# An encoder block on one core: the second norm's sum of squares moved to the end, and the operands of x made two blocks ahead

## The chip, the cores and the metric

One core of a Trainium2 chip runs the whole kernel. The metric is the device time of one execution in microseconds (us). Three runs of the kernel before took 1968.86, 1969.41 and 1969.3 us, median 1969.3 us. A further execution, the profiled one, took 1969.88 us, of which the profile's span from the first to the last instruction is 1968.2 us.

## What is computed

The input x is 512 tokens by 2048 channels in float32. Cut to what matters here:

```
u = rms_norm(x, mix_pre_gain)
p = u @ W_in                       (2048 x 5120)
mixed = concat(short gated convolution, conformer convolution with LayerNorm)
o = mixed @ W_out                  (2048 x 2048)
h = x + rms_norm(o, mix_post_gain)
m = rms_norm(h, mlp_pre_gain)      <- the second norm of this text
z = relu(m @ W_up)^2               (2048 x 8192)
out = h + rms_norm(z @ W_down, mlp_post_gain)
```

An rms_norm divides each token by the root of its mean square over the 2048 channels. This factor is one number per token, so it can be applied after a matmul. For the second norm it comes out as r^2 behind the square of the ReLU; the kernel multiplies by it only at the very end, as r^2 (`norm_2`) on the result and r^4 (`norm_4`) on the mean square under the last root.

## The kernel before, in words

Up to the last stage everything lies with channels across the 128 partitions and the 512 tokens along the free dimension; there are 16 blocks (k) of 128 channels. Each float32 operand is split into a high and a low part (`split`, lines 92 to 100: ScalarE writes the high part, VectorE the rest), and each product of two operands is three matmuls. Weights are split the same way by `Stationary.prepare` (lines 230 to 246: ScalarE line 237, VectorE line 242) from raw tiles of 128 x 1024 that the SP queue loads (line 122); there are six raw tiles. The order of instructions on every engine is the program's order (a manual schedule). All engines work through their own queue in that order.

**The first stage** is `k_major` (line 318) with `mixer_input` (line 448): four output tiles (PSUM banks) grow together, block by block of x. Per block k: x is split (lines 97 and 98), for even k below 8 a quarter of the first four weight tiles is cut into high and low parts (`cut_pieces`, lines 94 and 95), ScalarE squares x (line 409) and GpSimd adds the square to a running sum (line 405). From block 4 on, weight tiles 4 to 7, which are wanted from block 8 on, are prepared, one per block, behind the block's own operands. `together` (lines 309 to 316) issues twelve matmuls of 512 columns per block, three for each tile. `load_x` (line 442) loads a block of x four blocks ahead into one of eight buffers `tmp`, which x shares with the squares.

**The start of the MLP** (lines 729 to 760) does the same for h. Six blocks are done by half of the tokens; from block 6 on whole blocks follow. `residual` (lines 692 and 694, VectorE) makes h from x and o, `mlp_split` (lines 97 and 98) splits it, `together` multiplies it with the first four tiles of W_up. `keep_h` (line 710), up to two per block, writes h to memory, makes a scaled copy on ScalarE (line 713), and adds the square of h to `h_sum` (square on ScalarE line 409, sum on GpSimd lines 403 and 405). In blocks 12 to 15 one weight tile is prepared in each.

Behind it, in the first run of deferred work, `h_norm` (line 771) sums `h_sum` over the partitions by a matmul with ones (line 380) and takes the root.

**The last stage** has tokens across the partitions. Its last chunk works on tiles of 512 output channels (`wide_tile`, line 893): four banks, one per 128 tokens, four blocks, that is two steps of 24 matmuls. After each step `last_step` turns two pieces of h with four TensorE transposes each into one bank (`turn`, line 1005) and ScalarE copies the bank out (line 1013). `turn_norm` (line 997) turns r^2 the same way ahead of this. There are seven banks in all. After the four tiles, the second half of the chunk is worked row by row (line 1085), 128 tokens at a time, and each row ends with `last_sum`, `root` and `write`.

Of the kernel before, what the change touches and what calls it, by code (L numbers as in the profile page):

```python
# [8 lines left out]
F32 = mybir.dt.float32  # L9
F32R = mybir.dt.float32r  # L10
AF = mybir.ActivationFunctionType
ALU = mybir.AluOpType

P = 128
S = 512
TOK = S // 2
D = 2048
DA = 1024
FF = 8192
EPS = 1e-6  # L20
KT = D // P
# [9 lines left out]
START = 4  # L31
# [4 lines left out]
N_WIDE = D // WIDE  # L36
TB = S // P
# [21 lines left out]
def encoder_block(  # L59
    ctx: ExitStack, tc: tile.TileContext, x, par, gain, w_in, w_out, w_up, w_down, out  # L60
):
    nc = tc.nc
    pool = lambda name, bufs, **kw: ctx.enter_context(tc.tile_pool(name=name, bufs=bufs, **kw))
    const = pool("const", 1)
    stats = pool("stats", 2)
    small = pool("small", 12)
# [10 lines left out]
    new = lambda p, shape, dt, tag: p.tile(shape, dt, name=f"{tag}_{next(serial)}", tag=tag)  # L77
    scratch = lambda cols=S: new(tmp, [P, cols], F32, "tmp")
    slot = lambda shape, dt=F32: new(slots, shape, dt, "slot")
    bank = lambda cols=S: new(psum, [P, cols], F32, "bank")  # L80
# [6 lines left out]
    eps = const.tile([P, 1], F32, name="eps")  # L87
    nc.gpsimd.memset(eps, EPS)
    warm = const.tile([P, 1], F32, name="warm")
# [208 lines left out]
    def block(part, b):  # L298
        return tuple(w[:, b * P : (b + 1) * P] for w in part)

    def both(pair, cols=slice(0, S)):
        return pair[:, 0, cols], pair[:, 1, cols]

    def full_tile(parts, moving):
        ps = bank()
        products(ps, [(block(parts[k // HALF], k % HALF), both(moving[k])) for k in range(KT)])
        return ps

    def together(pss, parts, b, moving, first, last, cols=slice(0, S)):

        mhi, mlo = both(moving, cols)
        for ps, part in zip(pss, parts):
            hi, lo = block(part, b)
            nc.tensor.matmul(ps[:, cols], hi, mhi, start=first, stop=False)  # L314
            nc.tensor.matmul(ps[:, cols], lo, mhi, start=False, stop=False)  # L315
            nc.tensor.matmul(ps[:, cols], hi, mlo, start=False, stop=last)  # L316

    def k_major(n, make_moving, blocks=KT):

        pss = [bank() for _ in range(n)]  # L320
        for k in range(blocks):
            b = k % HALF
            if b == 0:
                parts = W.take(n, 0)
            moving = make_moving(k)
            if HALF // 2 <= b and b - HALF // 2 < n:
                W.prepare(W.taken + b - HALF // 2 + 1)
            together(pss, parts, b, moving, k == 0, k == blocks - 1)
        return pss

    lower, upper, every = slice(0, TOK), slice(TOK, S), slice(0, S)
    add = lambda out, a, b, op=ALU.add: nc.vector.tensor_tensor(out, a, b, op=op)  # L332
    pending = deque()

    def run_pending():
        while pending:
            pending.popleft()()
# [38 lines left out]
    def column_sums(tiles, cols=S):  # L376

        ps = new(psum_stat, [P, S], F32, "sums")
        for n, t in enumerate(tiles):
            nc.tensor.matmul(ps[:, :cols], ones, t, start=n == 0, stop=n == len(tiles) - 1)  # L380
        return ps[:, :cols]

    def inverse_root(ps, count, cols=S, out=None):

        y, v = scratch(cols), scratch(cols)
        nc.scalar.activation(y, ps, AF.Abs_reciprocal_sqrt, scale=1.0 / count, bias=eps)
        nc.vector.tensor_scalar(
            out=v, in0=ps, scalar1=1.0 / count, scalar2=EPS, op0=ALU.mult, op1=ALU.add
        )
        nc.vector.scalar_tensor_tensor(out=v, in0=v, scalar=-0.5, in1=y, op0=ALU.mult, op1=ALU.mult)  # L390
        nc.vector.tensor_tensor(v, v, y, op=ALU.mult)
        r = new(stats, [P, cols], F32, "rstd") if out is None else out
        nc.vector.scalar_tensor_tensor(out=r, in0=v, scalar=1.5, in1=y, op0=ALU.add, op1=ALU.mult)
        return r

    class Sum:
# [3 lines left out]
        def add(self, t):  # L400
            if self.total is None:
                self.total = new(stats, [P, self.cols], F32, "sum")
                nc.gpsimd.tensor_copy(self.total, t)
            else:
                nc.gpsimd.tensor_tensor(self.total, self.total, t, op=ALU.add)  # L405
# [55 lines left out]
    nc.scalar.dma_start(par_sb[:, KT:], par[:, KT:])  # L461
    W.load(START + 2)
    u = []
    pss = k_major(START, mixer_input)
    W.ahead = 5
    x_sums = column_sums([x_sum.total])
    for name, n in (("conv_b_w", TAPS_B * NB), ("ln_b_gain", NB), ("ln_b_bias", NB)):
        t = par_sb[:, _PAR[name] : _PAR[name] + n]
# [3 lines left out]
    norm = {}  # L472
# [115 lines left out]
    for kind, j, m in in_plan[START:]:  # L588
        parts = W.take(2, 2)
        run_pending()  # L590
        pump_sums()
        ps = full_tile(parts, u)
# [45 lines left out]
    pss = k_major(START, mixed_input)  # L638
    for m, ps in enumerate(pss):
        evacuate(keep_output, m, ps, scratch())  # L640
    for m in range(START, OUT_SEVEN[0]):
        parts = W.take(2, 2)
        run_pending()
        ps = full_tile(parts, mixed)
# [7 lines left out]


    h_dram = dram.tile([P, KT * S], F32, name="h_dram")
    h_sum = Sum()
    xr, rstd_o, mlp_in = [], {"all": new(stats, [P, S], F32, "rstd")}, {}

    def load_xr(k):
# [51 lines left out]
    def keep_h(k):  # L710
        h = xr[k // 2][:, k % 2, :]
        nc.scalar.dma_start(h_dram[:, k * S : (k + 1) * S], h)
        nc.scalar.activation(o[k], h, AF.Copy, scale=col("mlp_pre_gain", k))
        h_sum.add_square(h)

    parts = W.take(4, START)
    run_pending()
# [12 lines left out]
    parts = W.take(START, 0)  # L730
    pss = [bank() for _ in range(START)]
# [16 lines left out]
    for k in range(HEAD, KT):  # L748
        b = k % HALF
        if b == 0:  # L750
            parts = W.take(START, 0)
# [13 lines left out]
    def relu_squared(m, value, out):  # L765

        nc.scalar.activation(out, value, AF.Relu)
        nc.scalar.activation(out, out, AF.Square)
        nc.scalar.dma_start(z_dram[:, m * S : (m + 1) * S], out)

    def h_norm():
        r = inverse_root(column_sums([h_sum.total]), D)
        norm["h 2"], norm["h 4"] = r, new(stats, [P, S], F32, "rstd")
        nc.vector.tensor_tensor(r, r, r, op=ALU.mult)
        nc.vector.tensor_tensor(norm["h 4"], r, r, op=ALU.mult)

    t12, t3, t4 = [], [], []

    def right_sums(i):
# [25 lines left out]
        "t4": lambda i: both(mlp_in[2 * i], upper),  # L805
    }

    late = [h_norm] + [lambda m=m, ps=ps: relu_squared(m, ps, scratch()) for m, ps in enumerate(pss)]
    for m in range(START, UP_PLAIN):
        parts = W.take(2, 2)  # L810
        run_pending()
        ps = full_tile(parts, mlp_in)
        pending.extend(late)
        late = []
        pending.append(lambda m=m, ps=ps: relu_squared(m, ps, scratch()))
        n = HALF // (UP_PLAIN - START)
# [74 lines left out]
    tokens = lambda n: slice(n * P, (n + 1) * P)  # L891
# [60 lines left out]
    for c in range(N_CHUNK - 1):  # L952
        sums, waiting = deque(range(CHUNK // 2)), []
# [26 lines left out]
    identity = scratch(P)  # L980
    nc.gpsimd.memset(identity, 1.0)
    nc.gpsimd.affine_select(
        out=identity, in_=identity, pattern=[[1, P]], compare_op=ALU.is_equal, fill=0.0, base=0,
        channel_multiplier=-1,
    )
    norm_2, norm_4 = (new(small, [P, TB], F32, "four") for _ in range(2))
    h_raw, h_back = {}, {}

    def load_h(t):
# [4 lines left out]
            )  # L994
            h_raw[t, 2 * n], h_raw[t, 2 * n + 1] = pair[:, 0, :], pair[:, 1, :]

    def turn_norm():
        ps = bank()
        for b in range(TB):
            nc.tensor.transpose(ps[:, tokens(b)], norm["h 2"][:, tokens(b)], identity)  # L1000
        for b in range(TB):
            nc.scalar.activation(norm_2[:, b : b + 1], ps[:, b * P : b * P + 1], AF.Copy)
        add(norm_4, norm_2, norm_2, ALU.mult)

    def turn(t, b):

        if b % 2 == 0:
            pair = slot([P, 2, WIDE])
            h_back[t, b], h_back[t, b + 1] = pair[:, 0, :], pair[:, 1, :]
        ps = bank()  # L1010
        for i in range(4):
            nc.tensor.transpose(ps[:, tokens(i)], h_raw[t, i][:, tokens(b)], identity)  # L1012
        nc.scalar.activation(h_back[t, b], ps, AF.Copy)

    turns = deque((t, b) for t in range(N_WIDE) for b in range(TB))

# [8 lines left out]

    load_h(0)
    load_h(1)
    turn_norm()
    at = (N_CHUNK - 1) * CHUNK
    for t in range(N_WIDE):  # L1030
        wide_tile(t, False, range(at, at + CHUNK // 2), chunk_block, last_step)
# [9 lines left out]
    parts = {}  # L1041
# [1 line left out]
        for n in range(CHUNK // 4):  # L1043
            (parts[t, n],) = W.take(1, 1)
    run_pending()
    nc.scalar.activation(warm, eps, AF.Abs_reciprocal_sqrt)
    sums = [new(small, [P, N_WIDE], F32, "four") for b in range(TB)]

    def last_sum(b, t, ps, gained):
        v = total[t, b]  # L1050
# [4 lines left out]
        add(gained[t], v, gains[t // 2][:, t % 2, :], ALU.mult)  # L1055

    def root(b):
        mean, y, v, r = (new(small, [P, N_WIDE], F32, "four")[:, :1] for _ in range(4))
        nc.vector.tensor_reduce(out=mean, in_=sums[b], op=ALU.add, axis=mybir.AxisListType.X)
        add(mean, mean, norm_4[:, b : b + 1], ALU.mult)  # L1060
        nc.scalar.activation(y, mean, AF.Abs_reciprocal_sqrt, scale=1.0 / D, bias=eps)
        nc.vector.tensor_scalar(
            out=v, in0=mean, scalar1=1.0 / D, scalar2=EPS, op0=ALU.mult, op1=ALU.add
        )
        nc.vector.scalar_tensor_tensor(
            out=v, in0=v, scalar=-0.5, in1=y, op0=ALU.mult, op1=ALU.mult
        )
        nc.vector.tensor_tensor(v, v, y, op=ALU.mult)
        nc.vector.scalar_tensor_tensor(out=r, in0=v, scalar=1.5, in1=y, op0=ALU.add, op1=ALU.mult)
        add(r, r, norm_2[:, b : b + 1], ALU.mult)  # L1070
        return r

# [12 lines left out]
    for b in range(TB):  # L1085
        gained = {}
        for t in range(N_WIDE):
            run_pending()
            ps = bank()
            for i in range(CHUNK // 2):  # L1090
                k = CHUNK // 2 + i
# [88 lines left out]
```

## Time and profile before

| what | value |
|---|---|
| median of three runs | 1969.3 us |
| the profiled execution | 1969.88 us |
| its span | 1968.2 us |
| TensorE (matmul) busy | 1940.5 us, 99% |
| VectorE busy | 1542.1 us, 78% |
| ScalarE busy | 815.5 us, 41% |
| GpSimd busy | 99.8 us, 5% |
| share of TensorE in the chain that ended last | 95% |
| mean granted TensorE clock | 0.996 |

A matmul is pipelined and its end is modelled, so the durations of neighbours overlap: the pace is read from the starts. A DMA row tells the time of its issue, not of its landing. "Idle before" is the time in which an engine had nothing to do ahead of an instruction, and the name behind the arrow is what ended it.

### The profile page before, as it was taken

To read this page: it belongs to the slowest core of one execution; us is meant where nothing else is said; L and a number is where in the kernel's file an instruction comes from. 1 tells how busy PE (TensorE), PEld (TensorE's weight loads), DVE (VectorE), ACT (ScalarE), POOL (GpSimd) and SP (SyncE) were. 2 spreads that over 40 slices of the span, in tenths; PEclk is the share of its full clock that TensorE was granted. 3 is DMA by queue.
4 is the path that set the end of the run, shared out by engine and by line. 5 is a ranking of instruction groups with operands and counts; after the bars stand their busy time and mean duration, and the time that the engine had idled before them with its cause. 6 is when DMAs were issued, how large, how long until landed. Compare 5 with 4: busy or idle time off the path is not lost.

```text
span 1968.2 us, 28036 instructions
## 1 busy us (share of the span) xinstructions
PE 1940.5 (99%) x11224; PEld 1717.5 (87%) x11224; DVE 1542.1 (78%) x2000; ACT 815.5 (41%) x1091; POOL 99.8 (5%) x86
## 2 busy tenths in 40 slices
PE   8999999999999899999999999999999999999998
PEld 6888888888999689999999999988888888888886
DVE  7899989668786978777777777766777777777858
ACT  6222112353444654545444544546343333433332
POOL 4000010300210400000000000000000000000000
PEclk9999999999999999999999999999999999999999
DMA  8232323232446533434334343456262453634632
GB/s 255 86 112 86 107 86 107 87 117 75 125 145 228 189 123 113 160 109 145 124 124 145 111 158 108 161 182 207 81 225 99 158 187 111 216 102 155 218 124 86
DMA packets 85523, 272.54 MB, mean 138 GB/s; under 512 B 9616, under 2 KB 11792, under 8 KB 85392
## 3 DMA queue, kind: packets, MB, share of 16 engines
q1 hardware_dynamic: 71568, 245.92, 37.4%
q10 hardware_dynamic: 13824, 24.82, 3.3%
q8 instruction: 88, 1.44, 0.3%
q14 instruction: 43, 0.35, 0.0%
HBM read 241.87 MB, written 28.84 MB: 138 GB/s over the span
## 4 chain that ended last, share of the span: by engine, by line
PE 95%; DVE 3%; DMA 1%; issue 0%; ACT 0%; SPq 0%; ACTq 0%; DVEq 0%
PE bank L296 57%; PE bank L888 11%; PE bank L889 11%; PE bank L887 11%; PE bank L316 2%; PE bank L315 2%; PE bank L314 1%; DVE slot L694 1%; DVE slot L692 1%; DMA raw<-w_in_in 0%; DVE slot L242 0%; PE bank L1012 0%; PE sums L380 0%; DVE slot L98 0%; DMA tmp<-x_in 0%
## 5 line engine op out<-in xcount | busy, mean ns | idle before, releaser
L296 PE MATMUL bank<-slot,slot 128*128 128x256 f32 (+1 forms) x7584 | 1128.2, 311 | 0.0
L296 PEld LDWEIGHTS bank<-slot,slot 128*128 128x128 f32 x7584 | 1047.0, 191 | 80.6 <-issue 1.9
L242 DVE TENSOR_TENSOR slot<-raw,slot 128x1024 fp32r<-128x1024 f32 x332 | 412.7, 1260 | 57.0 <-ACT slot L237 50.7
L237 ACT ACTIVATE slot<-raw 128x1024 fp32r<-128x1024 f32 x332 | 338.0, 1049 | 143.2 <-DVE raw L212 67.4
L887 PE MATMUL bank<-slot,slot 128*128 128x512 f32 x968 | 377.6, 390 | 0.1
L888 PE MATMUL bank<-slot,slot 128*128 128x512 f32 x968 | 376.7, 389 | 0.2 <-DVE slot L95 0.2
L889 PE MATMUL bank<-slot,slot 128*128 128x512 f32 x968 | 376.8, 389 | 0.0
L237 ACT ACTIVATE slot<-slot 128x1024 fp32r<-128x1024 f32 x170 | 176.8, 1056 | 284.3 <-PE bank L296 161.1
L242 DVE TENSOR_TENSOR slot<-slot,slot 128x1024 fp32r<-128x1024 f32 x170 | 210.8, 1240 | 56.7 <-PE bank L887 38.5
L888 PEld LDWEIGHTS bank<-slot,slot 128*128 128x128 f32 x968 | 181.7, 188 | 38.0 <-DVE slot L95 0.5
L889 PEld LDWEIGHTS bank<-slot,slot 128*128 128x128 f32 x968 | 181.7, 188 | 37.8
L887 PEld LDWEIGHTS bank<-slot,slot 128*128 128x128 f32 x968 | 181.7, 188 | 37.7 <-ACT slot L94 0.3
L332 DVE TENSOR_TENSOR tmp<-tmp,bank 128x256 f32<-128x256 f32 x224 | 93.8, 419 | 112.5 <-PE bank L296 111.4
L94 ACT ACTIVATE slot<-tmp 128x512 fp32r<-128x512 f32 x96 | 54.1, 607 | 274.6 <-DVE tmp L332 144.3
L498 DVE SCALAR_TENSOR_TENSOR slot<-slot,par_sb,slot 128x512 f32<-128x512 f32 x240 | 162.9, 742 | 0.0
L332 DVE TENSOR_TENSOR slot<-slot,bank 128x512 f32<-128x512 f32 x164 | 106.0, 681 | 22.2 <-PE bank L889 22.1
L316 PE MATMUL bank<-slot,slot 128*128 128x512 f32 (+1 forms) x216 | 82.4, 381 | 9.6 <-DVE slot L98 9.6
L314 PE MATMUL bank<-slot,slot 128*128 128x512 f32 (+1 forms) x216 | 82.3, 381 | 8.0 <-ACT slot L94 8.0
L95 DVE TENSOR_TENSOR slot<-slot,slot 128x512 fp32r<-128x512 f32 (+1 forms) x80 | 49.6, 659 | 45.6 <-ACT slot L94 45.6
L405 POOL TENSOR_TENSOR sum<-sum,tmp 128x512 f32<-128x512 f32 x50 | 77.7, 1554 | 118.4 <-ACT tmp L409 116.9
L315 PE MATMUL bank<-slot,slot 128*128 128x512 f32 (+1 forms) x216 | 81.5, 377 | 0.3 <-DVE slot L95 0.3
L165 DVE TENSOR_TENSOR slot<-raw,raw 128x1024 f32<-128x1024 f32 x64 | 78.0, 1219 | 0.0
(102 smaller groups left out, 961.1 us busy)
## 6 DMA issues: line engine op xcount, KB each, us to landing
raw<-w_up_in SPq DMA_DIRECT2D x128, 512.0 KB, 5.3
raw<-w_down_in SPq DMA_DIRECT2D x128, 512.0 KB, 4.6
raw<-w_in_in SPq DMA_DIRECT2D x76, 512.0 KB, 4.0
slot<-z_dram SPq DMA_DIRECT2D x60, 512.0 KB, 6.4
raw<-w_out_in SPq DMA_DIRECT2D x32, 512.0 KB, 4.3
z_dram<-tmp ACTq DMA_DIRECT2D x64, 256.0 KB, 5.4
tmp<-x_in SPq DMA_DIRECT2D x16, 256.0 KB, 4.1
slot<-x_in SPq DMA_DIRECT2D x8, 512.0 KB, 7.6
```

The lines of the kernel that those rows point to most:

```text
L165: nc.vector.tensor_tensor(s[name], a, b, op=op)
L237: nc.scalar.activation(hi, value, AF.Copy)
L242: nc.vector.tensor_tensor(lo, value, hi.bitcast(F32), op=ALU.subtract)
L296: nc.tensor.matmul(ps, s, m, start=n == 0, stop=n == len(todo) - 1)
L314: nc.tensor.matmul(ps[:, cols], hi, mhi, start=first, stop=False)
L315: nc.tensor.matmul(ps[:, cols], lo, mhi, start=False, stop=False)
L316: nc.tensor.matmul(ps[:, cols], hi, mlo, start=False, stop=last)
L332: add = lambda out, a, b, op=ALU.add: nc.vector.tensor_tensor(out, a, b, op=op)
L498: nc.vector.scalar_tensor_tensor(out=acc, in0=g[:, k : k + S], scalar=w, in1=acc, op0=ALU.mult, op1=ALU.add)
L887: nc.tensor.matmul(ps, z_hi, lo, start=first, stop=False)
L888: nc.tensor.matmul(ps, z_lo, hi, start=False, stop=False)
L889: nc.tensor.matmul(ps, z_hi, hi, start=False, stop=last)
```

## The change

The second norm: `keep_h` no longer squares and sums h, and `h_norm` and `turn_norm` go. In `turn`, ScalarE, besides the copy, squares the turned bank with an accumulated sum into one column of `h_sums`. Ahead of the rows these 16 columns are summed, and the root is taken by small VectorE operations (`narrow_root`, whose code was in `root` and now serves both).

The first stage: `k_major` gets a parameter `lead`. With `lead=2`, as the first stage calls it, the operands of blocks k+1 and k+2 are issued ahead of the matmuls of block k and ahead of its preparation of a weight tile. The call for W_out keeps a lead of 0.

```diff
-    def k_major(n, make_moving, blocks=KT):
+    def k_major(n, make_moving, lead=0):
-        pss = [bank() for _ in range(n)]
-        for k in range(blocks):
+        pss, made = [bank() for _ in range(n)], []
+        for k in range(KT):
             b = k % HALF
             if b == 0:
                 parts = W.take(n, 0)
-            moving = make_moving(k)
+            while len(made) < min(k + 1 + lead, KT):
+                made.append(make_moving(len(made)))
+            moving = made[k]
             if HALF // 2 <= b and b - HALF // 2 < n:
                 W.prepare(W.taken + b - HALF // 2 + 1)
...
-    pss = k_major(START, mixer_input)
+    pss = k_major(START, mixer_input, 2)
...
         nc.scalar.activation(o[k], h, AF.Copy, scale=col("mlp_pre_gain", k))
-        h_sum.add_square(h)
...
-    def h_norm():
-        r = inverse_root(column_sums([h_sum.total]), D)
-        norm["h 2"], norm["h 4"] = r, new(stats, [P, S], F32, "rstd")
-        nc.vector.tensor_tensor(r, r, r, op=ALU.mult)
-        nc.vector.tensor_tensor(norm["h 4"], r, r, op=ALU.mult)
...
+    h_sums = scratch(TB * N_WIDE)
...
-    def turn_norm():
-        ps = bank()
-        for b in range(TB):
-            nc.tensor.transpose(ps[:, tokens(b)], norm["h 2"][:, tokens(b)], identity)
-        for b in range(TB):
-            nc.scalar.activation(norm_2[:, b : b + 1], ps[:, b * P : b * P + 1], AF.Copy)
-        add(norm_4, norm_2, norm_2, ALU.mult)
...
         nc.scalar.activation(h_back[t, b], ps, AF.Copy)
+        at = b * N_WIDE + t
+        nc.scalar.activation(scratch(), ps, AF.Square, accum_out=h_sums[:, at : at + 1])
...
-    nc.scalar.activation(warm, eps, AF.Abs_reciprocal_sqrt)
...
+    def narrow_root(mean):
+        y, v = (new(small, [P, N_WIDE], F32, "four")[:, : mean.shape[-1]] for _ in range(2))
+        nc.scalar.activation(y, mean, AF.Abs_reciprocal_sqrt, scale=1.0 / D, bias=eps)
...
+    norm_2, norm_4, h_mean = (new(small, [P, TB], F32, "four") for _ in range(3))
+    over_tiles(h_mean, h_sums.rearrange("p (b t) -> p b t", b=TB))
+    h_root = narrow_root(h_mean)
+    add(norm_2, h_root, h_root, ALU.mult)
+    add(norm_4, norm_2, norm_2, ALU.mult)
```

## Rows read from the trace of the kernel before

**Rows 1.** TensorE's timeline, start of the MLP, whole blocks: start us, us, instruction.

```profile
646.08 0.39 PE L314 MATMUL bank<-slot,slot 128*128 128x512 f32 x1
...
669.60 0.80 PE L316 MATMUL bank<-slot,slot 128*128 128x512 f32 x1 [3.03 <-DVE slot L98]
...
675.31 0.41 PE L314 MATMUL bank<-slot,slot 128*128 128x512 f32 x1
...
682.84 11.04 PE L296 MATMUL bank<-slot,slot 128*128 128x512 f32 x48
```

**Rows 2.** VectorE by line and shape, 639.4 to 643.5 us: busy us, mean ns.

```profile
L242 DVE TENSOR_TENSOR slot<-raw,slot 128x1024 fp32r<-128x1024 f32 x2 | 2.4, 1218 | 0.0
L692 DVE TENSOR_TENSOR slot<-slot,rstd 128x512 f32<-128x512 f32 x2 | 1.4, 685 | 0.0
L694 DVE SCALAR_TENSOR_TENSOR slot<-slot,par_sb,slot 128x512 f32<-128x512 f32 x1 | 0.7, 746 | 0.0
L98 DVE SCALAR_TENSOR_TENSOR slot<-slot,par_sb,slot 128x512 fp32r<-128x512 f32 x1 | 0.7, 746 | 0.0
```

**Rows 3.** The same view, 644.5 to 664.8 us.

```profile
L694 DVE SCALAR_TENSOR_TENSOR slot<-slot,par_sb,slot 128x512 f32<-128x512 f32 x6 | 10.0, 1663 | 0.0
L692 DVE TENSOR_TENSOR slot<-slot,rstd 128x512 f32<-128x512 f32 x5 | 8.9, 1779 | 0.0
L98 DVE SCALAR_TENSOR_TENSOR slot<-slot,par_sb,slot 128x512 fp32r<-128x512 f32 x5 | 3.7, 739 | 0.0
```

**Rows 4.** GpSimd's timeline in that stretch.

```profile
646.67 3.19 POOL L405 TENSOR_TENSOR sum<-sum,tmp 128x512 f32<-128x512 f32 x2 [0.88 <-ACT tmp L409]
```

**Rows 5.** ScalarE by line, 644.5 to 664.8 us: busy us, mean ns, idle before.

```profile
L97 ACT ACTIVATE slot<-slot,par_sb 128x512 fp32r<-128x512 f32 x5 | 3.6, 725 | 4.8 <-DVE slot L694 4.8
```

**Rows 6.** The chain that ended last, in order of time: start us, us, what.

```profile
693.88 0.86 PE sums L380 x2
...
1863.98 0.44 PE bank L1000 x4
```

**Rows 7.** TensorE's timeline in the first stage.

```profile
24.21 0.39 PE L316 MATMUL bank<-slot,slot 128*128 128x512 f32 x1
...
30.33 0.39 PE L316 MATMUL bank<-slot,slot 128*128 128x512 f32 x1
```

**Rows 8.** ScalarE's timeline in the first stage.

```profile
24.42 1.06 ACT L237 ACTIVATE slot<-raw 128x1024 fp32r<-128x1024 f32 x1 [2.90 <-DMA raw<-w_in_in]
```

**Rows 9.** Loads of x blocks 5 to 8: first and last issue, time to landing.

```profile
L442 SPq DMA_DIRECT2D tmp<-x_in x4: 430/546/608, 13.3 to 15.1; - x4
DMA to landing us min/median/max: 6.7/6.8/6.9
```

**Rows 10.** VectorE's timeline in the first stage.

```profile
26.79 1.42 DVE L95 TENSOR_TENSOR slot<-raw,slot 128x256 fp32r<-128x256 f32 x4
...
31.02 2.32 DVE L242 TENSOR_TENSOR slot<-raw,slot 128x1024 fp32r<-128x1024 f32 x1
33.26 7.57 DVE L98 SCALAR_TENSOR_TENSOR slot<-tmp,par_sb,slot 128x512 fp32r<-128x512 f32 x5
```

**Rows 11.** TensorE's timeline at the end of a wide tile.

```profile
1888.79 1.03 PE L1012 MATMUL bank<-tmp,slot 128*128 128x128 f32 x8
...
1890.35 0.39 PE L887 MATMUL bank<-slot,slot 128*128 128x512 f32 x1
...
1891.03 0.39 PE L887 MATMUL bank<-slot,slot 128*128 128x512 f32 x1
```

**Rows 12.** ScalarE's timeline, the same turn, and a square with accumulated sum in the rows.

```profile
1889.42 1.09 ACT L1013 ACTIVATE slot<-bank 128x512 f32<-128x512 f32 x2 [4.33 <-PE bank L1012]
...
1923.46 0.64 ACT L1053 ACTIVATE tmp<-slot 128x512 f32<-128x512 f32 x1 [4.57 <-DVE slot L332]
1924.00 0.19 ACT L1053 ACTIVATION_READ_ACCUMULATOR tmp<-slot 128x1 f32 x1
```

**Rows 13.** VectorE's timeline, first tile of the last row.

```profile
1950.63 0.69 DVE L332 TENSOR_TENSOR slot<-slot,bank 128x512 f32<-128x512 f32 x1 [1.28 <-PE bank L889]
```

More of the change, by code (lines that the diff above doesn't have):

```diff
@@ L324, in k_major @@
                 parts = W.take(n, 0)
-            moving = make_moving(k)
+            while len(made) < min(k + 1 + lead, KT):
+                made.append(make_moving(len(made)))
+            moving = made[k]
             if HALF // 2 <= b and b - HALF // 2 < n:
                 W.prepare(W.taken + b - HALF // 2 + 1)
-            together(pss, parts, b, moving, k == 0, k == blocks - 1)
+            together(pss, parts, b, moving, k == 0, k == KT - 1)
         return pss
@@ L654, in encoder_block @@
     h_dram = dram.tile([P, KT * S], F32, name="h_dram")
-    h_sum = Sum()
     xr, rstd_o, mlp_in = [], {"all": new(stats, [P, S], F32, "rstd")}, {}
@@ L806, in encoder_block @@
     }
-    late = [h_norm] + [lambda m=m, ps=ps: relu_squared(m, ps, scratch()) for m, ps in enumerate(pss)]
+    late = [lambda m=m, ps=ps: relu_squared(m, ps, scratch()) for m, ps in enumerate(pss)]
     for m in range(START, UP_PLAIN):
@@ L985, in encoder_block @@
     )
-    norm_2, norm_4 = (new(small, [P, TB], F32, "four") for _ in range(2))
+    h_sums = scratch(TB * N_WIDE)
     h_raw, h_back = {}, {}
@@ L1027, in encoder_block @@
     load_h(1)
-    turn_norm()
     at = (N_CHUNK - 1) * CHUNK
@@ L1045, in encoder_block, with over_tiles @@
     run_pending()
-    nc.scalar.activation(warm, eps, AF.Abs_reciprocal_sqrt)
     sums = [new(small, [P, N_WIDE], F32, "four") for b in range(TB)]
+    def narrow_root(mean):
+        y, v = (new(small, [P, N_WIDE], F32, "four")[:, : mean.shape[-1]] for _ in range(2))
+        nc.scalar.activation(y, mean, AF.Abs_reciprocal_sqrt, scale=1.0 / D, bias=eps)
+        nc.vector.tensor_scalar(
+            out=v, in0=mean, scalar1=1.0 / D, scalar2=EPS, op0=ALU.mult, op1=ALU.add
+        )
+        nc.vector.scalar_tensor_tensor(
+            out=v, in0=v, scalar=-0.5, in1=y, op0=ALU.mult, op1=ALU.mult
+        )
+        add(v, v, y, ALU.mult)
+        nc.vector.scalar_tensor_tensor(out=v, in0=v, scalar=1.5, in1=y, op0=ALU.add, op1=ALU.mult)
+        return v
+    def over_tiles(out, sums):
+        nc.vector.tensor_reduce(out=out, in_=sums, op=ALU.add, axis=mybir.AxisListType.X)
+    norm_2, norm_4, h_mean = (new(small, [P, TB], F32, "four") for _ in range(3))
[3 more added lines that the diff above has]
+    add(norm_4, norm_2, norm_2, ALU.mult)
     def last_sum(b, t, ps, gained):
@@ L1057, in root @@
     def root(b):
-        mean, y, v, r = (new(small, [P, N_WIDE], F32, "four")[:, :1] for _ in range(4))
-        nc.vector.tensor_reduce(out=mean, in_=sums[b], op=ALU.add, axis=mybir.AxisListType.X)
+        mean = new(small, [P, N_WIDE], F32, "four")[:, :1]
+        over_tiles(mean, sums[b])
         add(mean, mean, norm_4[:, b : b + 1], ALU.mult)
[L1061 to L1069, printed above, removed]
+        r = narrow_root(mean)
         add(r, r, norm_2[:, b : b + 1], ALU.mult)
```

## The prediction

> **What bounds the kernel now.** I read the table of busy shares first: TensorE is busy 99% of the span, so the change can only gain where it takes matmuls away or closes one of the few stretches in which matmuls do not follow each other at full pace. I looked for these in TensorE's timeline. At full clock, in a stretch without waits, 33 matmuls of 512 columns start between 675.31 and 682.84 us, 0.228 us each [rows 1]. There are two slow stretches.
>
> At the start of the MLP, blocks 7 to 15 are nine blocks of twelve matmuls, 108 in all. They take from 646.08 to 682.84, 36.76 us, where 108 x 0.228 = 24.6 us would do [rows 1]. So 12.1 us are lost there. What ends the longest wait is VectorE's line 98, the low part of h. VectorE has no idle time in this stretch [rows 3], so it sets the pace. Per block it does lines 692, 98 and 694. While GpSimd is still, these take 0.69, 0.75 and 0.75 us [rows 2]; in the slow stretch line 692 takes 1.78 us and line 694 1.66 us, and line 98 alone stays at 0.74 [rows 3]. GpSimd's sums of squares come two at a time for 3.19 us with 0.88 us of rest before [rows 4]; line 98 falls into the rest. So each sum of h costs VectorE about 1.78 - 0.69 = 1.09 us.
>
> In the first stage, 72 matmuls (six blocks) have started by 24.21 us, and the ninth after it starts at 30.33 [rows 7]: 6.12 us for nine steps of 0.228, 4.1 us lost. ScalarE waits there for the DMA of a raw weight tile until 24.42 [rows 8], and the parts of x block 6 are queued behind it.
>
> **The change, part by part.**
>
> *The sums of h at the MLP's start go* (16 squares on ScalarE, 16 GpSimd operations). The squares were not on the path: ScalarE idled before line 97 waiting for VectorE [rows 5]. The GpSimd sums were on it, through VectorE. Without them a block of VectorE is at most 0.75 + 0.73 (ScalarE's line 97, longer than line 692 that runs beside it) + 0.75 = 2.23 us [rows 2, 5], against 12 x 0.228 = 2.74 us of matmuls. TensorE becomes the bound. Blocks 7 to 11 gain VectorE 5 x 0.5 = 2.5 us of lead. Blocks 12 to 15 carry a weight tile's low part, 1.22 us [rows 2]: 0.69 + 0.75 + 0.75 + 1.22 = 3.41, that is 4 x 0.67 = 2.7 us of lead used up, so it is just enough. I take the whole 12.1 us. Bounds: 12.1 us, and 6.7 us, if TensorE waits out all 2.7 us of blocks 12 to 15 and the clock falls behind that wait once more (2.75 us, below).
>
> *`h_norm` goes*: one sum over the partitions on TensorE, 0.86 us [rows 6]. Its root on ScalarE and VectorE held up nobody on TensorE: nothing.
>
> *`turn_norm` goes*: four transposes, 0.44 us [rows 6]. Its four copies and one product are beside the matmuls: nothing.
>
> *Sixteen squares with an accumulated sum come into the last stage*, two per step. Each is 0.54 us to its read of the accumulator and 0.19 us for that, 0.73 us [rows 12]; ScalarE idles 4.33 us per step before the copies [rows 12], so its own time is covered. If the cover were gone it would be 16 x 0.73 = 11.7 us. What is not covered is the bank: it is free only after the square. There are seven banks, four belong to the tile, and if they are handed out in the order in which they come free, the next tile's second and third banks are those of the last two turns. At the tile end at 1888.79 the next tile wants its second bank at 1890.35 and its third at 1891.03 [rows 11]. The first copy starts at 1889.42 and two take 1.09 [rows 12]. With the square behind each copy the first bank is free at 1889.42 + 0.55 + 0.73 = 1890.70, 0.35 us late, and the second 1.28 us later at 1891.98, against 1891.03 + 0.35 = 1891.38: 0.60 us late. That is 0.95 us at each of three boundaries (at the fourth, rows follow, which want one bank every 2.7 us): 2.8 us lost. Bounds: nothing, if other banks are handed out, and 4 us. I take 2.8.
>
> *The root of h comes ahead of the rows.* Some nine operations on a few columns, at the 0.19 us of the nearest row (the accumulator's read [rows 12]) 1.7 us, and weight parts that come 2 x 0.73 us later behind the squares push VectorE back by 3.2 us at the first row; the bounds are nothing and twice that. VectorE waits 1.28 us for TensorE at the first tile of the last row [rows 13], and likewise in the two rows before it, 3.8 us in all: this covers it, and the tail is unchanged; at twice the price 2.6 us would show. `warm` goes: nothing.
>
> *x two blocks ahead.* On SP two more loads of x (blocks 9 and 10) go ahead of weight tile 6. x block 5 is issued at 13.3 and lands 6.7 us later at 20.0 [rows 9], so its low part starts after ScalarE's 0.73 at 20.7. Block 6, whose parts now go before weight tiles 4 to 7, is then in time, and the wait of rows 7 and 8 goes. But the weights are later. Tile 6 now takes a buffer that the last cut frees, which comes behind x block 6. And VectorE has, ahead of the low part of tile 7, which block 8 needs: x blocks 5 to 9 (5 x 0.75), four cuts (1.42), four weight tiles (4 x 1.22). That is 10.0 us by durations, 9.2 us by starts (31.02 + 2.32 overlaps the next by 0.08) [rows 2, 10]. Between them come five or six of GpSimd's sums for x, 1.09 us each [rows 2, 3]. Tile 7 is ready at 20.7 + 9.2 + 5.5 = 35.4, or 36.4 with six. TensorE would want it after blocks 6 and 7 and ten more matmuls, at 24.4 + 34 x 0.228 = 32.2 [rows 7]. Block 9 can start two matmuls after it, at 35.9 or 36.9. Before, it started 28 matmuls after 30.33, at 36.7. So the wait moves from block 6 to block 8, and the gain is 0.3 us in the middle. After a long wait the clock falls: behind the 3.03 us wait, 13 matmuls took 5.71 us instead of 2.96, 2.75 us more [rows 1]. Here, after the new wait, I take 1.5 of it. Sum: 1.2 us lost. Bounds: 4.1 us gained (no wait at all) and 3.0 us lost.
>
> The Trainium skill bears on the sums (SBUF — State Buffer, § "Who interferes with whom"): VectorE instructions with two SBUF inputs and GpSimd instructions share one port, and whoever comes first keeps it for its whole instruction. By it a sum could cost VectorE its whole 1.6 us instead of 1.09, and six of them in the first stage 3 us more; the rows speak for 1.09.
>
> **The sum**: -12.1 - 0.86 - 0.44 + 2.8 + 1.2 = -9.4 us. The profiled execution (1969.88 us, 1.7 us of it outside its span) would come to 1960.5; the median of the three runs lies 0.6 us below it, so 1959.9 us.
>
> **The rivals.**
>
> *The first stage gains in full.* VectorE and GpSimd interleave better than I count, or block 8 is not held up: 4.1 us gained instead of 1.2 lost, 1959.9 - 5.3 = 1954.6. For it: one sum more or less moves the result by 1.1 us. Against it: VectorE has no slack from 20.7 on. Chance 0.2.
>
> *VectorE stays half the bound at the MLP's start*: the weight parts of blocks 12 to 15 hold up TensorE, between nothing and the bound of 5.4 us less gained; with the clock's 2.75 and half of the 2.7, 4.1 us: 1964.0. For it: the lead of 2.5 us against 2.7 used. Against: starts lie closer than durations. Chance 0.12.
>
> *Slower.* Lines 692 and 694 are long for a reason of their own (the stores of h, ScalarE reading the same tiles) and not by GpSimd's sums. The place is blocks 7 to 15, the price the whole 12.1 us: 1959.9 + 12.1 = 1972.0. It decides if VectorE's block without the sums stays over 2.74 us by more than a third. Against it: line 98 in the same stretch is short, and the same lines were short just before [rows 2, 3]. Chance 0.04.
>
> **How the numbers follow.** My forecast has 0.62; what it leaves uncertain (boundaries 0 to 4, first stage within 1.5) gives 1956.5 to 1962.5. About 0.2%, 3.9 us, is what a measurement of this kernel can tell from no change. The range takes in most of the first two rivals: 1954.3 to 1963.8. Faster than 1965.4 are the forecast, the first rival and nearly all of the second: 0.93. Within 0.2%: 0.04, from the second's worst bounds. Slower by over 0.2% (above 1973.2) needs the third rival with the first stage at its bound: 0.03 with what I have not thought of.
>
> **What would show it.** In the profile after: lines 692 and 694 at 0.69 and 0.75 us throughout the MLP's start, blocks 7 to 15 in about 24.6 us at full clock, no GpSimd sum in it, and TensorE's waits for line 98 down to those of the half blocks. In the first stage no wait at block 6 but one of 3 to 4 us at block 8 for line 242, with the clock down behind it, and line 380 at about 57 us. At each tile end in the last stage two waits of some 0.4 us for the square in `turn`. Wrong would be: line 692 still above 1.5 us; no wait at block 8; no wait at the tile ends.

## The result and the profile after

| | before | after |
|---|---|---|
| median | 1969.19 us (4 runs) | 1958.73 us (4 runs, 1957.65 to 1961.33) |
| the profiled execution | 1969.88 us | 1959.29 us |
| its span | 1968.2 us | 1957.6 us |
| GpSimd busy | 99.8 us | 75.4 us |
| mean granted TensorE clock | 0.996 | 0.997 |

The ratio is 0.9949, with a 95% interval of 0.9932 to 0.9966: faster, by 10.5 us. The forecast was 1959.9 us in a range of 1954.3 to 1963.8.

To see where the time went, the same piece of work is looked up in both timelines of TensorE, and its start before is subtracted from its start after. Where the difference moves, time was won or lost. (Lines move a little: 692 and 694 are now 694 and 696, 380 is 383, 1012 and 1013 are 999 and 1000; the new square is line 1002.)

| work | before | after | after minus before |
|---|---|---|---|
| first matmul behind the first stage (L296) | 56.20 | 56.89 | +0.69 |
| MLP block 7, first matmul | 646.08 | 646.77 | +0.69 |
| first matmul behind block 15 (L296) | 682.84 | 671.25 | -11.59 |
| first turn of h | 1869.72 | 1856.73 | -12.99 |
| first turn behind the third tile end | 1907.82 | 1897.17 | -10.65 |
| last matmul of all | 1958.37 | 1947.72 | -10.65 |

So: +0.69 in the first stage, -12.28 at the MLP's start, -1.40 for the two matmul groups of `h_norm` and `turn_norm` that are gone, +2.34 at the tile ends and nothing in the rows.

**The MLP's start.** TensorE's timeline of the kernel after, answering [rows 1] (start us, us, instruction; some lines):

```profile
644.37 0.50 PE L316 MATMUL bank<-slot,slot 128*128 128x512 f32 x1 [0.91 <-DVE slot L98]
...
646.77 0.39 PE L314 MATMUL bank<-slot,slot 128*128 128x512 f32 x1
...
671.25 28.95 PE L296 MATMUL bank<-slot,slot 128*128 128x512 f32 x127
```

Blocks 7 to 15 take 671.25 - 646.77 = 24.48 us instead of 36.76, and no wait is left in them: the last one, 0.91 us, is in block 6. That is 0.227 us for each of the 108 matmuls, the pace of a full clock. VectorE by line and shape, 644.5 to 664.8 us, answering [rows 3] (busy us, mean ns, idle before):

```profile
L98 DVE SCALAR_TENSOR_TENSOR slot<-slot,par_sb,slot 128x512 fp32r<-128x512 f32 x8 | 6.0, 749 | 1.6 <-ACT slot L97 1.6
L696 DVE SCALAR_TENSOR_TENSOR slot<-slot,par_sb,slot 128x512 f32<-128x512 f32 x8 | 6.0, 746 | 0.0
L694 DVE TENSOR_TENSOR slot<-slot,rstd 128x512 f32<-128x512 f32 x8 | 5.5, 686 | 0.0
L242 DVE TENSOR_TENSOR slot<-raw,slot 128x1024 fp32r<-128x1024 f32 x3 | 3.7, 1219 | 0.0
```

The two lines that took 1.78 and 1.66 us take 0.69 and 0.75, as in [rows 2]. VectorE now does eight blocks and three weight parts in the time of five blocks, and even idles 1.6 us. GpSimd has no instruction here, so nothing answers to [rows 4].

**The first stage.** TensorE, answering [rows 7]:

```profile
35.20 0.50 PE L315 MATMUL bank<-slot,slot 128*128 128x512 f32 x1 [1.79 <-DVE slot L242]
...
36.17 0.63 PE L315 MATMUL bank<-slot,slot 128*128 128x512 f32 x1
...
38.73 0.61 PE L315 MATMUL bank<-slot,slot 128*128 128x512 f32 x1
...
56.44 1.02 PE L383 MATMUL sums<-sum,ones 128*128 128x512 f32 x2
```

The wait of 1.85 us at block 6 is gone, and one of 1.79 us stands at block 8, for the low part of weight tile 7. Behind it the six steps from 36.17 to 38.73 take 0.43 us each, against 0.23 at full pace. That is the lower of the clock's two levels, 1.2 in place of 2.4 GHz (granted clock from 36 to 39 us: 0.50). The sums start at 56.44; before it was 55.74.

The stage also begins differently in the two traces, first the kernel after, then the kernel before:

```profile
7.59 0.63 PE L316 MATMUL bank<-slot,slot 128*128 128x512 f32 x1
...
11.86 0.42 PE L314 MATMUL bank<-slot,slot 128*128 128x512 f32 x1
```

```profile
7.52 0.63 PE L316 MATMUL bank<-slot,slot 128*128 128x512 f32 x1
...
9.66 0.44 PE L315 MATMUL bank<-slot,slot 128*128 128x512 f32 x1
```

Ten steps of 0.43 us stand here after the change and five before it. This brings TensorE to block 8 some 1.0 us later. The granted clock is recorded as 1.00 in both stretches, so no row says what held the pace. In all the traces of this text there are 4 to 10 such steps with a lead and 4 to 6 without; whether the lead has a part in them is open.

**The tile ends.** TensorE at the end of a wide tile, answering [rows 11]:

```profile
1876.55 1.04 PE L999 MATMUL bank<-tmp,slot 128*128 128x128 f32 x8
1877.34 0.47 PE L882 MATMUL bank<-slot,slot 128*128 128x512 f32 x1
...
1878.41 0.50 PE L882 MATMUL bank<-slot,slot 128*128 128x512 f32 x1
...
1879.47 0.50 PE L882 MATMUL bank<-slot,slot 128*128 128x512 f32 x1
```

and ScalarE at the same turn, answering [rows 12]:

```profile
1877.18 0.60 ACT L1000 ACTIVATE slot<-bank 128x512 f32<-128x512 f32 x1 [3.15 <-PE bank L999]
1877.68 0.59 ACT L1002 ACTIVATE tmp<-bank 128x512 f32<-128x512 f32 x1
1878.15 0.20 ACT L1002 ACTIVATION_READ_ACCUMULATOR tmp<-bank 128x1 f32 x1
1878.24 0.60 ACT L1000 ACTIVATE slot<-bank 128x512 f32<-128x512 f32 x1
1878.72 0.61 ACT L1002 ACTIVATE tmp<-bank 128x512 f32<-128x512 f32 x1
1879.20 0.22 ACT L1002 ACTIVATION_READ_ACCUMULATOR tmp<-bank 128x1 f32 x1
```

The second and third bank of the next tile begin 1.86 and 2.92 us after the turn; before, it was 1.56 and 2.24 [rows 11]. The two starts fall 0.06 and 0.05 us behind the ends of the two reads, at 1878.35 and 1879.42.

**The rows.** VectorE's wait for TensorE, answering [rows 13], is the only one left of three:

```profile
1939.98 0.69 DVE L335 TENSOR_TENSOR slot<-slot,bank 128x512 f32<-128x512 f32 x1 [0.99 <-PE bank L884]
```

### The profile page after: what moved, and what is told of

It reads as the page before. It is cut to its first block, busy times and chain, and to the rows that moved or that the text cites. A ratio compares the mean times of both kernels' runs of the same rounds, so it can differ in the third digit from the quotient of the medians.

```text
span 1957.6 us, 28019 instructions
## 1 busy us (share of the span) xinstructions
PE 1936.3 (99%) x11218; PEld 1716.1 (88%) x11218; DVE 1522.6 (78%) x2000; ACT 815.9 (42%) x1102; POOL 75.4 (4%) x70
## 4 chain that ended last, share of the span: by engine, by line
PE 96%; DVE 2%; DMA 1%; ACT 1%; issue 0%; SPq 0%; ACTq 0%; DVEq 0%
PE bank L296 57%; PE bank L882 11%; PE bank L883 11%; PE bank L884 11%; PE bank L315 2%; PE bank L316 2%; PE bank L314 2%; DVE slot L242 1%; DMA tmp<-x_in 1%; PE bank L999 0%; DVE slot L98 0%; PE sums L383 0%; DVE slot L1077 0%; DMA raw<-w_in_in 0%; DMA par_sb<-par_in 0%
## 5 line engine op out<-in xcount | busy, mean ns | idle before, releaser
L296 PE MATMUL bank<-slot,slot 128*128 128x256 f32 (+1 forms) x7584 | 1127.6, 311 | 0.0
L296 PEld LDWEIGHTS bank<-slot,slot 128*128 128x128 f32 x7584 | 1047.0, 191 | 80.1 <-issue 1.4
L95 DVE TENSOR_TENSOR slot<-tmp,slot 128x512 fp32r<-128x512 f32 x96 | 60.3, 666 | 29.6 <-ACT slot L94 29.4
```

What stands on the lines that cost most here:

```text
L95: nc.vector.tensor_tensor(lo, value, hi.bitcast(F32), op=ALU.subtract)
L296: nc.tensor.matmul(ps, s, m, start=n == 0, stop=n == len(todo) - 1)
```

## The experiments

The theory: the GpSimd sums of h cost the 12 us, through VectorE; the lead in the first stage only moves a wait; the tile ends lose their time to a bank that the square holds. The rivals are in the expectations. Where a time is set against "after", the two may be of different sets of runs; each set had the kernel before beside it, with 15 runs (medians 1969.98 and 1969.85).

**The lead alone.** Two kernels are the one after with another lead, one is the kernel before with `k_major` of the change and a lead of 2.

```diff
-    pss = k_major(START, mixer_input, 2)
+    pss = k_major(START, mixer_input, 0)
```

With a lead of 0:

> The changed kernel with a lead of 0: x is made as before, the second norm as after. Theory (the lead only moves the wait from block 6 to block 8): the first stage is back to its wait of about 1.9 us before block 6 for ScalarE's line 94, line 383 starts about 0.7 us earlier than in the changed kernel, and the time is 0.7 us shorter than the changed kernel's, about 1958 us. Rival (the lead gains in full and something else gave it back): 3 to 4 us longer, about 1962 us.

Measured: 1958.85 us (5 runs), ratio 0.9942 [0.9929, 0.9956]. In the trace a wait of 0.93 us for line 94 is back at block 6, the clock does not fall behind it, and the sums start at 55.92 us, 0.52 earlier than in the kernel after.

With a lead of 1:

> The changed kernel with a lead of 1. Theory (what counts is how much VectorE and GpSimd work lies ahead of the low part of weight tile 7): one block of x and one sum less, 1.7 us, lie ahead of it than with a lead of 2, so the wait in block 8 shrinks to about 0.5 us, but block 7's x is behind weight tile 6 in ScalarE's queue and waits about 1.3 us; the first stage ends 0.5 to 1.5 us earlier than with a lead of 2. Rival (the wait in block 8 comes from the late raw tile alone): the wait in block 8 stays at about 1.8 us.

Measured: 1959.51 us (5 runs), ratio 0.9946 [0.9934, 0.9959]. In the trace the wait for line 242 is down to some 0.3 us (its matmul starts at 36.13 us, 0.53 behind the one before, where full pace is 0.23), near the 0.5 expected, and this speaks against a late raw tile alone. But 1.37 us for line 97 stand at block 7 and 0.51 us for line 98 at block 9, and the sums start at 56.53 us, not 0.5 to 1.5 earlier than with a lead of 2 but 0.09 later.

The kernel before with the lead alone:

```diff
-    pss = k_major(START, mixer_input)
+    pss = k_major(START, mixer_input, 2)
```

> The kernel before with a lead of 2 alone; the second norm as before. Theory: 0.7 us slower than before, about 1969.9 us, with the wait in block 8 for line 242 and the clock down behind it. Rival (the lead gains in full): 1965 us.

Measured: 1969.72 us (11 runs, 1968.79 to 1971.3) against 1969.98, ratio 1.0001 [0.9992, 1.001]. None of the three differs from its counterpart by a microsecond (1958.73 with a lead of 2, 1969.98 without), nor do the gains over the kernel before of the same set (10.46 us with a lead of 2, 11.13 with 0, 10.47 with 1). So neither a gain nor a loss of that size by the lead is borne out. The trace of this last run, whose profiled execution was the fastest of the eleven, shows how the 0.69 us of the first stage is to be read. TensorE's timeline there:

```profile
35.06 0.50 PE L315 MATMUL bank<-slot,slot 128*128 128x512 f32 x1 [1.62 <-DVE slot L242]
...
54.69 1.02 PE L383 MATMUL sums<-sum,ones 128*128 128x512 f32 x2
```

The wait sits at the same place and is of the same size as in the kernel after, but the sums start 1.75 us earlier. What differs is the clock behind the wait. Busy time by stretch (us; busy and count of PE, PEld, DVE, ACT and POOL; granted clock; DMA share; GB/s), first in the kernel after:

```profile
35.00:45.00 10.00, 9.80 (x36) 7.95 (x37) 10.00 (x7) 9.13 (x14) 9.53 (x8) 0.83 0.84 290
```

and in the kernel before with the lead:

```profile
35.00:45.00 10.00, 9.94 (x44) 8.24 (x45) 9.59 (x8) 9.99 (x15) 8.94 (x6) 1.00 0.83 288
```

At 0.83, 36 matmuls fit into the ten microseconds; at 1.00 it is 44, eight times 0.228 = 1.8 us more. With the clock down the lead loses 0.7 us against the kernel before; without it, 54.69 stands against 55.74. But the trace of the kernel before has its own fall of the clock, behind its wait at block 6:

```profile
26.45 0.50 PE L314 MATMUL bank<-slot,slot 128*128 128x512 f32 x1 [1.85 <-ACT slot L94]
...
27.86 0.63 PE L316 MATMUL bank<-slot,slot 128*128 128x512 f32 x1
```

The six steps from 27.86 to 30.33 [rows 7] take 0.41 us each, 1.1 us more than at full pace, as much as those 1.05 us. Among the traces without a fall the sums start at 54.69 and 55.62 us with a lead of 2 (here and with the square on the copy, below) and at 55.11, 55.21 and 55.92 with none (copies first and GpSimd's sums left out, both below, and the lead of 0). The two groups overlap, so the traces show no gain by the lead either.

**GpSimd's sums left out, ScalarE's squares kept**, in the kernel before:

```diff
-        h_sum.add_square(h)
+        sq = h_sum.square(h)
+        if k == 0:
+            h_sum.add(sq)
```

> The kernel before, with ScalarE's squares of h kept and GpSimd's running sum taken for the first block alone (the sum of squares of h is left incomplete). My theory: GpSimd's adds alone stretch VectorE's lines 692 and 694; without them these take 0.69 and 0.75 us, blocks 7 to 15 of the MLP's first gate take about 24.5 us in place of 36.8, the one-matmul waits of 0.8 and the 3.0 us wait are gone, and the whole takes about 1957.5 us. Rival: ScalarE's squares, queued ahead of the evictions that VectorE waits for, are what was late; then the stretch stays near 36 us and the time near 1969.

Measured: 1959.35 us (4 runs), ratio 0.9948 [0.9934, 0.9962]. VectorE, 644.5 to 664.8 us:

```profile
L98 DVE SCALAR_TENSOR_TENSOR slot<-slot,par_sb,slot 128x512 fp32r<-128x512 f32 x7 | 5.3, 751 | 4.3 <-ACT slot L97 4.3
L694 DVE SCALAR_TENSOR_TENSOR slot<-slot,par_sb,slot 128x512 f32<-128x512 f32 x7 | 5.2, 745 | 0.0
L692 DVE TENSOR_TENSOR slot<-slot,rstd 128x512 f32<-128x512 f32 x7 | 4.8, 683 | 0.0
```

The lines 692 and 694 are short again, so it was GpSimd's adds that stretched them. But blocks 7 to 15 take 672.35 - 645.51 = 26.84 us, 2.36 more than without the squares, and the total is 1.9 us above the 1957.5 expected. Here the rival had a part: with GpSimd out of the way the squares become a bound, and VectorE now waits 4.3 us for ScalarE's line 97, against 1.6 in the kernel after. Busy time by stretch (columns as above):

```profile
652.00:658.00 6.00, 6.00 (x26) 4.54 (x25) 4.26 (x8) 6.00 (x11) 0.00 (x0) 1.00 0.62 230
658.00:664.00 6.00, 5.50 (x22) 3.60 (x20) 5.32 (x8) 6.00 (x11) 0.00 (x0) 1.00 0.59 184
```

The fourth busy time is ScalarE's: 6.00 of 6.00. In the kernel after it is 5.47 and 4.99 in the same stretches, without the squares of 0.62 us each.

**GpSimd's sums put back, without squares**, in the kernel after (the blocks of h themselves are added; the sum is used by nobody):

```diff
+    h_sum = Sum()
...
+        h_sum.add(h)
```

> The kernel after, with a running sum on GpSimd of the blocks of h themselves (one add of 128x1024 per block; no squares on ScalarE, the sum is not used, the output is the same). My theory: GpSimd's adds bring lines 694 and 696 back to about 1.7 us on VectorE, blocks 7 to 15 back to 34 to 37 us, and the time to about 1969 to 1971. Rival (the squares on ScalarE made the delay): no more than 1 us slower than the kernel after, 1959.

Measured: 1971.49 us (10 runs), ratio to before 1.0005 [0.9995, 1.0014], 12.8 us above the kernel after. From the sums of the first stage to the first matmul behind block 15 it takes 683.59 - 56.65 = 626.94 us, against 671.25 - 56.44 = 614.81 in the kernel after: 12.1 us, all of the difference of the spans but 0.3. The theory had the total right and two details wrong, so the agreement of the total with the 12.28 us is in part luck. Blocks 7 to 15 take 683.59 - 654.70 = 28.9 us, not 34 to 37, and 7.7 of the 12.1 us are lost ahead of them: the sums (of 128x512, not 128x1024) run one per block, beginning with block 0, and blocks 3 to 6 already wait 1.64, 1.64, 1.90 and 1.66 us, where the kernel after waits 0.56, 0.57, 0.83 and 0.91. And the instruction that is stretched is another one. GpSimd's timeline:

```profile
636.39 2.12 POOL L408 TENSOR_TENSOR sum<-sum,slot 128x512 f32<-128x512 f32 x1 [0.83 <-DVE slot L697]
...
651.07 1.61 POOL L408 TENSOR_TENSOR sum<-sum,slot 128x512 f32<-128x512 f32 x1 [2.02 <-DVE slot L697]
```

VectorE's timeline in the same places:

```profile
636.17 1.21 DVE L242 TENSOR_TENSOR slot<-raw,slot 128x1024 fp32r<-128x1024 f32 x1
637.30 1.48 DVE L695 TENSOR_TENSOR slot<-slot,rstd 128x256 f32<-128x256 f32 x1
...
651.72 1.51 DVE L98 SCALAR_TENSOR_TENSOR slot<-slot,par_sb,slot 128x512 fp32r<-128x512 f32 x1 [0.19 <-ACT slot L97]
```

It is whichever VectorE instruction comes next behind the add: here line 98, there line 695. The line has nothing to do with it.

**The sums of x left out**, in the kernel after:

```diff
-        x_sum.add_square(xs[k])
+        sq = x_sum.square(xs[k])
+        if k == 0:
+            x_sum.add(sq)
```

> The kernel after, with ScalarE's squares of x kept and GpSimd's running sum of x taken for the first block alone (the first norm is left incomplete, so the output differs). Theory of the first stage: VectorE's share of the last x tiles is late because GpSimd's adds stretch it; without them the wait of 1.8 us at block 8 shrinks to under 0.5 us and line 383 starts 2 to 4 us earlier, total 1955 to 1957. Rival: the late landing of the raw tiles sets that wait; then it stays over 1 us and the time within 1 us of 1958.8.

Measured: 1956.17 us (4 runs), ratio 0.993 [0.9917, 0.9944], 2.6 us below the kernel after. TensorE:

```profile
33.75 0.50 PE L315 MATMUL bank<-slot,slot 128*128 128x512 f32 x1 [0.63 <-DVE slot L242]
...
53.38 1.02 PE L383 MATMUL sums<-sum,ones 128*128 128x512 f32 x2
```

VectorE's weight part for tile 7 in this kernel:

```profile
32.48 1.22 DVE L242 TENSOR_TENSOR slot<-raw,slot 128x1024 fp32r<-128x1024 f32 x1
```

and in the kernel after:

```profile
32.84 2.30 DVE L242 TENSOR_TENSOR slot<-raw,slot 128x1024 fp32r<-128x1024 f32 x1
```

The sums start 3.06 us earlier. The wait falls from 1.79 to 0.63 us, a little over the 0.5 expected, and the clock does not fall behind it. The start of the part hardly moves (32.48 against 32.84): without the sums VectorE waits just ahead of it, 0.86 us for ScalarE's line 97, and ScalarE had waited 0.55 us for a raw tile. So the late tiles have a share in the wait that is left, but the length of the part, 1.22 or 2.30 us, is GpSimd's.

**Where the square reads.** In the kernel after the square reads the copy in SBUF instead of the bank:

```diff
-        nc.scalar.activation(scratch(), ps, AF.Square, accum_out=h_sums[:, at : at + 1])
+        nc.scalar.activation(scratch(), h_back[t, b], AF.Square, accum_out=h_sums[:, at : at + 1])
```

> The changed kernel with the square taken from the copy of h in SBUF and not from the PSUM bank. Theory (the bank is held by the square): at the three tile ends the second and third bank come without a wait, and the steps of the last stage are all 6.35 us as before; 0.8 us gained at each of three ends, 2.4 us in all, about 1956.3 us. Rival (TensorE waits there for something else, the weight parts or VectorE's evacuation behind ScalarE's longer queue): the waits stay and the time is that of the changed kernel.

Measured: 1957.29 us (5 runs), ratio 0.9939 [0.9926, 0.9951]. From one tile end to the next it takes 1882.07 - 1868.99 = 13.08 us instead of 1883.69 - 1870.21 = 13.48; before it was 1895.12 - 1882.42 = 12.70. So half of the loss of 0.78 us is gone. The other half is the order: the second copy still stands behind the first square. TensorE at the turn:

```profile
1875.33 1.04 PE L999 MATMUL bank<-tmp,slot 128*128 128x128 f32 x8
...
1876.89 0.40 PE L882 MATMUL bank<-slot,slot 128*128 128x512 f32 x1
...
1877.85 0.50 PE L882 MATMUL bank<-slot,slot 128*128 128x512 f32 x1
```

The second bank comes 1.56 us after the turn, as before the change, the third 2.52 us after it.

**Copies first, then squares**, and no lead:

```diff
-    pss = k_major(START, mixer_input, 2)
+    pss = k_major(START, mixer_input, 0)
...
+    def square(t, b):
...
-        nc.scalar.activation(scratch(), ps, AF.Square, accum_out=h_sums[:, at : at + 1])
+        nc.scalar.activation(scratch(), h_back[t, b], AF.Square, accum_out=h_sums[:, at : at + 1])
...
-            turn(*turns.popleft())
+        two = [turns.popleft() for _ in range(2)]
+        for tb in two:
+            turn(*tb)
+        for tb in two:
+            square(*tb)
```

> The kernel after, with no block of lead, and the two copies of a turn ahead of its two squares, which read the copy in SBUF instead of the bank. Theory (a bank of the turn is held by the square behind the copy): the three tile ends lose their 0.8 us each, so the time falls by 2.3 us against the kernel after, to about 1956.4; where the order of the squares does nothing beyond their operand, it falls by 1.1 to 1.2. Rival (the tile end loses its time to the turn's matmuls, as it may have before): no gain beyond 0.2 us.

Measured: 1956.54 us (5 runs, 1955.85 to 1956.75), ratio 0.9931 [0.9919, 0.9944], 2.3 us below the same kernel with the squares on the bank (1958.85). TensorE at the turn:

```profile
1874.48 1.04 PE L999 MATMUL bank<-tmp,slot 128*128 128x128 f32 x8
...
1876.05 0.40 PE L882 MATMUL bank<-slot,slot 128*128 128x512 f32 x1
...
1876.73 0.40 PE L882 MATMUL bank<-slot,slot 128*128 128x512 f32 x1
```

and ScalarE:

```profile
1875.11 1.09 ACT L1000 ACTIVATE slot<-bank 128x512 f32<-128x512 f32 x2 [3.08 <-PE bank L999]
1876.09 0.64 ACT L1004 ACTIVATE tmp<-slot 128x512 f32<-128x512 f32 x1
```

The banks come 1.57 and 2.25 us after the turn, and a tile takes 12.70 us (1880.84 - 1868.14), both as before the change. The loss at the tile ends is thus settled, and this version is faster than both kernels.

## Why the prediction was right, point by point

**The MLP's start** (-12.1): -12.28 in the trace. The cause that it named, GpSimd's sums through VectorE, is shown from both sides: taken out of the kernel before, the lines become short; put into the kernel after, 12.1 us come back, though in part at other blocks. Its sentence that the squares were not on the path holds for the kernel before alone: with the sums gone and the squares kept, ScalarE is full and costs 2.4 us. It did not matter, since both went. The lead of VectorE over blocks 12 to 15, "just enough", was enough: no wait there. So the rival in which VectorE stays half the bound fell, and the slower one, by which the lines were long for a reason of their own, fell with the short lines.

**`h_norm` and `turn_norm`** (-0.86 - 0.44 = -1.30): -1.40 between the matmul behind block 15 and the first turn.

**The tile ends** (+2.8): +2.34 in the table of offsets, 2.3 by the last experiment. The mechanism was right, the banks in the order in which they come free included; the size was too large in one term. A copy and a square with its read were put at 0.55 + 0.73 = 1.28 us per turn; the starts lie 1.06 us apart (1877.18 to 1878.24), since the next copy starts 0.09 us after the read does, not at its end. So the second bank was 0.30 us late and the third 0.68 (the sum said 0.35 and 0.95).

**The first stage** (+1.2): +0.69 in the two profiles, and the wait moved from block 6 to block 8 as said. Tile 7 was ready at 32.84 + 2.30 = 35.14 us (35.4 in the working). The wait was 1.79 us, not 3 to 4: TensorE came to it later than the 32.2 us of the working, at 35.20 - 1.79 = 33.4, and 1.0 us of that is the slower start of the stage in this trace, which the working did not count. The 1.5 us for the clock was about what the fall cost here. But as a term of the median this step was too precise. Of the five traces with a lead of 2 the clock falls there in two (the kernel after, and the one with GpSimd's sums put back) and in three it does not, and the medians with a lead of 0, 1 and 2 (1958.85, 1959.51, 1958.73) don't differ by more than they scatter. So the 0.69 us belongs to these two executions, and by the medians the term is zero within a microsecond.

**The root ahead of the rows** (nothing, by 3.8 us of cover): the three waits of VectorE for TensorE, 0.68, 1.28 and 1.28 us before, are down to one of 0.99. That is 2.25 us of cover used, and the rows lose nothing: the last matmul keeps the 10.65 us of the third tile end. The cover that the prediction counted was 3.24 us and not 3.8, since the first of the three is shorter than it took from [rows 13].

**The sum** was -9.4 us against -10.6 of span. The losses were put 1.0 us too high (4.0 against 2.34 + 0.69), and the gains 0.3 too low (13.4 against 12.28 + 1.40). That the median came within 1.2 us of the forecast is in part luck, since the four executions alone lie 3.7 us apart.

## What to carry to other kernels

An engine that is hardly busy can set the pace of a whole stage through another engine: when VectorE's instructions of one shape have two durations in one trace, look at what GpSimd does in the places of the long ones, and move that work to an engine that has room. A second reader of a PSUM bank costs as much as it delays the bank's release, and only where the next matmuls want that very bank: do all copies out first, and read the copy. And a wait that sits behind other late work need not go when its operands are issued earlier: here it appeared at the next operand.

## What the runs showed of the hardware that was not expected

**Sums and VectorE take strict turns.** In the rows with GpSimd's sums put back, VectorE's line 242 ends at 636.17 + 1.21 = 637.38 us. GpSimd's add, which started at 636.39, ends at 638.51, 1.13 us after that; and VectorE's next instruction, of 256 columns, which began at 637.30, ends at 638.78, 0.27 us after the add. So the add's 2.12 us contain nearly 1 us in which it waits for VectorE, and its own work is about 1.13 us; the nine other adds between 632 and 662 us end 1.13 to 1.15 us behind the VectorE instruction that ran as they began. That is about the price that VectorE pays: 2.30 against 1.22 us, 1.08 more, for the part of tile 7. The Trainium skill says that the first to come keeps the port for its whole instruction (SBUF — State Buffer, § "Who interferes with whom"), and the trace agrees. The prediction set the rule's price at the add's whole recorded 1.6 us, against 1.09 from the rows; the rows were right, and the rule was misread: a recorded duration on GpSimd includes its own wait.

**The clock falls behind some waits and not behind others of the same length.** In the first stage it fell to half rate behind one of 1.79 us (the kernel after: granted clock 0.50 from 36 to 39 us) and one of 1.90 us (GpSimd's sums put back: 0.50 from 37 to 40), and stayed at 1.00 behind one of 1.62 us (the kernel before with the lead) and behind two of 0.69 and 1.91 us (the square on the copy: 1.00 from 36 to 40). What decides it was not tried. In the kernel after, eight steps behind the wait take 0.2 us more each, 1.6 us, which is more than the lead moved any median.
